# Head 0's gate and value projections interleaved, x staged later: a two-layer retention and latent-attention trunk

## The chip, the cores and the metric

The kernel runs on one core of a Trainium2 chip. The metric is the device time of one execution in microseconds (us), the median of several runs. A separate execution is recorded by the hardware profiler; all views of the profile come from that one. Five engines work side by side, each in its own order: TensorE (PE in the profile, with PEld for its weight loads), VectorE (DVE), ScalarE (ACT), GpSimd (POOL) and SyncE (SP), which issues most of the DMA transfers.

## What is computed

A trunk of two layers over 256 positions with 2048 features, all in float32. Layer one is retention with 8 heads and a squared-ReLU MLP, layer two is multi-head latent attention (MLA) with 16 heads over one shared set of keys and values, and a second MLP. The part that the change touches is the start of the retention and the end of the shared keys:

```python
h = rms_norm(x, norm_mix[layer])
proj = h @ w_in
q, k, v, gate = jnp.split(proj, ...)              # 8 heads: q, k of 256, v, gate of 512
q, k = apply_rope(q, ...), apply_rope(k, ...) * dk ** -0.5
o = ...                                           # decayed causal q k^T v, per head
o = o * lax.rsqrt(jnp.mean(o * o, axis=-1, keepdims=True) + RMS_EPS)
x = x + (jax.nn.silu(gate) * o) @ w_out
...
kv = (c_kv @ w_kv_up).reshape(b, s, MLA_HEADS, MLA_NOPE_DIM + MLA_V_DIM)
k_nope = rms_norm(kv[..., :MLA_NOPE_DIM], k_nope_norm)
```

## The kernel before

**Tiling.** The 256 positions are two row tiles of 128 (`t`), the 2048 features are 16 row blocks of 128 (`k`), paired into 8 chunks (`c`, two blocks `j` each). To keep float32 precision every operand is split into a high and a low part: ScalarE casts the high part (`split`, L191, or with a scale L194) and VectorE subtracts it to get the low one (L192, L195). A product then takes three matmuls: high by high, high by low, low by high (L252 to L254 for plain GEMMs, L376 to L378 for the later ones).

**Weights.** `stream` (L214) loads a 1 MB piece of a weight matrix into a `raw` tile (4 buffers), splits each half of it into `wh` and `wl` (5 buffers each) and hands the half to `use`, which issues the matmuls. `piece` (L241) does that for plain GEMMs, `gemm_t` (L261) for the transposed queries and keys, `gemm_pair` (L351) for the big ones.

**Normalisation.** The row factor of the first norm, `r0`, is applied after the projections, so they can start on the raw, transposed x (`xt`) times the gain. `first_inputs` (L592) loads one chunk of `xt` and splits it; chunks 2, 4, 5 and 7 are loaded again later for sums (`again`, L602). `load_x` (L620) loads x itself in blocks of 512 columns, takes the sum of squares on ScalarE and writes the block to its place in HBM (`x_home`) by a DMA that GpSimd issues.

**The order of head 0.** `gemm(..., "rg0", gated, start)` (L777) makes the gates over all 16 row blocks. It is given `start` (L627): before each half piece of weights one chunk of `xt` is loaded, for the first halves between two parts of the weight load. With half 3 also positions, constants (`cst`, 672 columns) and `gpe` are loaded, with half 5 GpSimd begins the rope tables (`ret_tables`, L570), with half 7 the loads of x and `scale_tables` (L574) are queued. Then `ret_projected` (L728) makes the queries (`rq0`) and the keys (`rk0`), and a second `gemm` makes the values (`rv0`, L779). `gated` copies the gates' sums to SBUF (L767) and applies the Silu 8 steps later; the values are read from PSUM by `ret_valued` (L739).

**What sets the order.** Work that isn't on the matmul path is put in a queue: `later(n, fn)` (L99) runs `fn` when the clock, which `tick` raises by one after each weight piece, has gone on by n. The rotation of queries and keys (`ret_rope`, L640), the scores (`ret_scores`, L660), the outputs (`ret_out`, L681) and the table transposes (`tr_tp`, L585) are timed in this way. Below that, the tile framework orders each engine's instructions by its own plan and puts in the waits: `gqn` (L1037) stands near the end of the code and runs at 4.56 us. Tiles of one tag share their buffers: `acc` has four PSUM banks (one GEMM takes two, L426), `f2k` 14 SBUF buffers.

**The last keys.** `keys(b)` (L1030) makes one eighth of the keys and values of MLA; seven are made before the queries, the eighth after them (L1160), and right behind it comes the output projection `wo` (L1165). `keyed` (L1000) empties the two accumulators with four ScalarE instructions (L1010, L1011), 128x256 each, scaled by `rc`.

Of the kernel before, what the change touches and what calls it, by code (L numbers as in the profile page):

```python
# [21 lines left out]
NT = 2  # L22
# [46 lines left out]
def yoco(ctx: ExitStack, tc: tile.TileContext, a):  # L69
# [144 lines left out]
    def stream(w, chunk, cols, name, use, done=None, before=None):  # L214

        raw = pool.tile([P, 2048], F32, tag="raw", bufs=4, name=f"{name}_raw")
        if before is None:
            nc.sync.dma_start(raw[:, :cols], w[chunk])
        n = cols // 2
        for half in range(2):  # L220
            wh = pool.tile([P, 1024], F32R, tag="wh", bufs=5, name=f"{name}_wh{half}")
            wl = pool.tile([P, 1024], F32R, tag="wl", bufs=5, name=f"{name}_wl{half}")
            cuts = 1
            if before is not None:
                cuts = 1 if half else 2
                m = n // cuts
                for i in range(cuts):
                    lo = half * n + i * m
                    nc.sync.dma_start(raw[:, lo : lo + m], w[chunk][:, lo : lo + m])
                    if i == 0:  # L230
                        before(half)
# [9 lines left out]
    def piece(w, chunk, acc, act, g, nk, nb, name, before=None, done=None):  # L241

        if before is None:
            need(act, 2 * g + 2)

        def use(half, wh, wl):
            for j in range(2):
                k = g * 4 + half * 2 + j
                rh, rl = (v[:, j * nb : (j + 1) * nb] for v in (wh, wl))
                for t in range(NT):  # L250
                    ah, al = (act[k // 2][:, j, i, t * P : (t + 1) * P] for i in range(2))
                    nc.tensor.matmul(acc[t], ah, rh, start=k == 0, stop=False)  # L252
                    nc.tensor.matmul(acc[t], ah, rl, start=False, stop=False)
                    nc.tensor.matmul(acc[t], al, rh, start=False, stop=k == nk - 1)  # L254

        stream(
            w, chunk, 4 * nb, f"{name}{g}", use, done and (lambda: done(acc)),
            before and (lambda half: before(2 * g + half)),
        )
# [169 lines left out]
    def gemm(w, chunk0, act, nk, nb, name, done, before=None):  # L429
# [3 lines left out]
        for g in range(n - 1):  # L433
            piece(w, chunk0 + g, acc, act, g, nk, nb, name, before)
        last_piece(w, chunk0, acc, act, nk, nb, name, done, before)

    def last_piece(w, chunk0, acc, act, nk, nb, name, done, before=None):
        g = nk // 4 - 1
        piece(w, chunk0 + g, acc, act, g, nk, nb, name, before, done)
# [64 lines left out]
    def sincos(inv, w, name, pos_f=pos_f):  # L504
# [37 lines left out]
        def finish(zero):  # L542
            sc = f2k([2, n], f"{name}_sc")
            nc.scalar.activation(sc, r, AF.Sin, bias=zero)
# [25 lines left out]
    def ret_tables():  # L570
        nc.vector.tensor_copy(pos_f, pos_i)
        ret_sc.append(sincos(cst[:, C_INVR : C_INVR + 128], 128, "tr"))

    def scale_tables():  # L574
# [4 lines left out]
        sc = ret_sc[0](zero)  # L579
# [10 lines left out]
    act0, sums0, r0, ret_sc, mla_sc, no_turn = [], [], [], [], [], []  # L590

    def first_inputs(c):  # L592

        t = f2k([2, S], f"x0t_{c}")
        nc.sync.dma_start(t, a["xt"][:, 2 * c : 2 * c + 2, :])
# [4 lines left out]
        if c in HEAD:  # L600
# [12 lines left out]
            later({2: 21, 4: 14, 5: 15, 7: 17}[c], again)  # L613
# [6 lines left out]
    def load_x(b):  # L620
        for t in range(NT):
# [3 lines left out]
            nc.gpsimd.dma_start(x_home[t][b], x0)  # L625

    def start(half):  # L627
        first_inputs(half)
        if half == 3:
# [3 lines left out]
        if half == 5:  # L633
            ret_tables()
        if half == 7:
            for b in range(NB):
                later(2 + b, lambda b=b: load_x(b))
            later(6, scale_tables)

    def ret_rope(acc, out, name, wait):  # L640

        u = f2k([2, S], f"{name}_u")
        for i in range(2):
# [37 lines left out]
    def ret_out(h, s, v, gate, y_act):  # L681
# [17 lines left out]
        if h == 0:  # L699
# [5 lines left out]
            later(25, mla_tables)  # L705
# [22 lines left out]
    def ret_projected(h, qk, gate, v, s):  # L728

        wait = 0 if h else 8  # L730

        def keyed(acc):
            ret_rope(acc, qk, f"rk{h}", max(wait - 4, 0))
            later(max(wait - 4, 0) + (2 if h else 1), ret_scores(h, qk, s))

        gemm_t(a["ret_w_qk"], h * 2, act0, KD, f"rq{h}", lambda acc: ret_rope(acc, qk, f"rq{h}", max(wait - 2, 0)))
        gemm_t(a["ret_w_qk"], (RH + h) * 2, act0, KD, f"rk{h}", keyed)

    def ret_valued(src, h, s, v, gate):  # L739
# [5 lines left out]
        later(1, lambda: ret_out(h, s, v, gate, halves[h // 4]))  # L745
# [14 lines left out]
    for h in range(RH):  # L760
        qk, gate, v, s = [], [], [], []
        if h == 0:

            def gated(acc, gate=gate):
                src = [f2k([512], f"gate_raw{t}") for t in range(NT)]
                for t in range(NT):
                    nc.scalar.copy(src[t], acc[t])  # L767

                def silu():
                    for t in range(NT):  # L770
                        g = f2k([512], f"gate0{t}")
                        nc.scalar.activation(g, src[t], AF.Silu, scale=r0[t])
# [6 lines left out]
            gemm(  # L779
                a["ret_w_gv0"], 4, act0, KD, 512, "rv0",  # L780
                lambda acc, v=v, s=s, gate=gate: ret_valued(acc, 0, s, v, gate),
            )
# [217 lines left out]
    def keyed(acc, b):  # L1000
# [6 lines left out]
        for t in range(NT):  # L1007
            src = acc[t].rearrange("p (h c) -> p h c", h=2)
            k = f2k([2, 2, NOPE], f"kn{b}{t}")
            nc.scalar.activation(k[:, 0], src[:, :, 0:NOPE], AF.Copy, scale=rc[t])  # L1010
# [260 lines left out]
```

## Time and profile before

| | |
|---|---|
| median of 3 runs | 2458.53 us (2458.52 to 2459.41) |
| the profiled execution | 2459.33 us, its span 2457.5 us |
| mean granted TensorE clock | 0.999 |
| busy | TensorE 100%, VectorE 90%, ScalarE 66%, GpSimd 10% |
| DMA | 522.10 MB, 212 GB/s over the span |
| first matmul of head 0's gates | 5.66 us |
| gates, then queries begin, values begin | 31.34, 53.92 us |

The span runs from the first to the last instruction; the time also holds what lies around it. In a timeline row stand the start, the busy time, engine, line, operation, output and inputs by the program's names, the count, and in brackets how long the engine had been idle before it and what released it. A row of the windows view has the stretch and its length, then for PE, PEld, DVE, ACT and POOL the busy time and the number of instructions, then the granted clock, the busy share of the DMA engines and their rate in GB/s; asked for one line of the code, only the engine that runs it is listed. A row of the waits view has the engine and line that waited, what for, the total, the times and the longest. Matmuls are pipelined: their durations overlap, and the distance of their starts is what one costs.

### The profile page before, as it was taken

The page shows a single profiled execution, that of the slowest core. Times are in us where ns is not written, and L with a number is a line of the kernel's source. Part 1 is how long each engine was busy: PE and PEld are TensorE (multiplying, and loading weights), DVE is VectorE, ACT ScalarE, POOL GpSimd, SP SyncE. Part 2 cuts the span into 40 slices and gives each one's busy share as a digit, 9 for nine tenths or more (in the row PEclk, how much of TensorE's full clock was granted, in tenths as well). Part 3 has the DMA queues.
Part 4 walks back from the last instruction along what each step waited for, and adds up shares of the span by engine and source line. Part 5 has one row for each costly group of instructions (what it writes and reads, how often), then busy time and mean ns, then how long its engine had stood idle before and what let it go on. Part 6 is the DMA issues. An engine that isn't in the chain of part 4 may idle for free.

```text
span 2457.5 us, 31830 instructions
## 1 busy us (share of the span) xinstructions
PE 2448.9 (100%) x11620; PEld 2057.4 (84%) x11620; DVE 2220.2 (90%) x2893; ACT 1629.1 (66%) x2300; POOL 250.0 (10%) x311
## 2 busy tenths in 40 slices
PE   9999999999999999999999999999999999999999
PEld 7888888888888888888888888998888888888887
DVE  7799999889899999999999998777999999999998
ACT  6566656566676667667666777676776666676665
POOL 7300011000010010110110001110000101101101
PEclk9999999999999999999999999999999999999999
DMA  9545568555564685674785565445555856857856
GB/s 335 207 174 208 189 208 244 193 183 216 201 237 178 211 261 212 208 257 180 242 271 202 183 223 184 156 150 180 206 189 197 259 212 208 271 197 226 262 188 188
DMA packets 93980, 522.10 MB, mean 212 GB/s; under 512 B 11136, under 2 KB 12288, under 8 KB 40576
## 3 DMA queue, kind: packets, MB, share of 16 engines
q1 hardware_dynamic: 70992, 471.25, 53.2%
q0 software_dynamic: 22400, 48.25, 9.1%
q8 instruction: 91, 1.49, 0.2%
q10 hardware_dynamic: 432, 0.57, 0.1%
q14 instruction: 65, 0.53, 0.1%
HBM read 479.14 MB, written 41.94 MB: 212 GB/s over the span
## 4 chain that ended last, share of the span: by engine, by line
PE 99%; ACT 0%; DVE 0%; DMA 0%; issue 0%; POOL 0%; SPq 0%; ACTq 0%; POOLq 0%
PE u_c L376 7%; PE u_c L378 7%; PE u_c L377 7%; PE d_c L376 7%; PE d_c L378 7%; PE d_c L377 7%; PE rp_c L376 3%; PE rp_c L377 3%; PE rp_c L378 3%; PE rk_acc L280 2%; PE rq_acc L280 2%; PE u_p L376 2%; PE u_p L377 2%; PE u_p L378 2%; PE d_p L376 2%; PE d_p L377 2%
## 5 line engine op out<-in xcount | busy, mean ns | idle before, releaser
L191 ACT CAST u_wh<-u_raw 128x1024 fp32r<-128x1024 f32 x360 | 345.9, 992 | 197.7 <-DVE u_raw L339 95.6
L191 ACT CAST d_wh<-d_raw 128x1024 fp32r<-128x1024 f32 x342 | 327.5, 990 | 185.4 <-DVE d_raw L339 93.9
L192 DVE TENSOR_TENSOR u_wl<-u_raw,u_wh 128x1024 fp32r<-128x1024 f32 x360 | 400.1, 1146 | 36.4 <-ACT u_wh L191 31.3
L192 DVE TENSOR_TENSOR d_wl<-d_raw,d_wh 128x1024 fp32r<-128x1024 f32 x342 | 378.5, 1142 | 30.8 <-ACT d_wh L191 26.2
L376 PE MATMUL u_c<-u_wh,n 128*128 128x512 f32 x712 | 278.8, 392 | 0.0
L377 PE MATMUL u_c<-u_wl,n 128*128 128x512 f32 x712 | 277.8, 390 | 0.0
L378 PE MATMUL u_c<-u_wh,n 128*128 128x512 f32 x712 | 277.4, 390 | 0.0
L376 PE MATMUL d_c<-d_wh,hid 128*128 128x512 f32 x654 | 256.0, 391 | 0.0
L377 PE MATMUL d_c<-d_wl,hid 128*128 128x512 f32 x654 | 255.3, 390 | 0.0
L378 PE MATMUL d_c<-d_wh,hid 128*128 128x512 f32 x654 | 254.8, 390 | 0.0
L191 ACT CAST rp_wh<-rp_raw 128x1024 fp32r<-128x1024 f32 (+1 forms) x166 | 158.8, 981 | 128.1 <-DVE rp_raw L339 65.2
L192 DVE TENSOR_TENSOR rp_wl<-rp_raw,rp_wh 128x1024 fp32r<-128x1024 f32 (+1 forms) x166 | 184.1, 1137 | 18.4 <-ACT rp_wh L191 16.5
L378 PEld LDWEIGHTS u_c<-u_wh,n 128*128 128x128 f32 x712 | 133.7, 188 | 27.7
L376 PEld LDWEIGHTS u_c<-u_wh,n 128*128 128x128 f32 x712 | 133.7, 188 | 27.2
L377 PEld LDWEIGHTS u_c<-u_wl,n 128*128 128x128 f32 x712 | 133.8, 188 | 26.7
L378 PEld LDWEIGHTS d_c<-d_wh,hid 128*128 128x128 f32 x654 | 122.8, 188 | 25.4
L376 PEld LDWEIGHTS d_c<-d_wh,hid 128*128 128x128 f32 x654 | 122.8, 188 | 25.0
L377 PEld LDWEIGHTS d_c<-d_wl,hid 128*128 128x128 f32 x654 | 122.9, 188 | 24.6
L156 POOL DMA_DIRECT2D xh<-d_c x52 | 45.1, 867 | 925.5 <-ACT d_c L396 923.6
L191 ACT CAST ro_wh<-ro_raw 128x1024 fp32r<-128x1024 f32 x88 | 85.6, 996 | 59.4 <-DVE ro_raw L339 25.2
L376 PE MATMUL rp_c<-rp_wh,a 128*128 128x512 f32 x286 | 111.8, 391 | 0.0
L377 PE MATMUL rp_c<-rp_wl,a 128*128 128x512 f32 x286 | 111.3, 389 | 0.0
(584 smaller groups left out, 6177.8 us busy)
## 6 DMA issues: line engine op xcount, KB each, us to landing
u_raw<-in_mlp_w SPq DMA_DIRECT2D x128, 1024.0 KB, 5.3
d_raw<-in_mlp_w SPq DMA_DIRECT2D x120, 1024.0 KB, 4.9
rp_raw<-in_ret_w_gv SPq DMA_DIRECT2D x56, 1024.0 KB, 4.9
ro_raw<-in_ret_w_out SPq DMA_DIRECT2D x32, 1024.0 KB, 4.9
uq_raw<-in_mla_w_uq SPq DMA_DIRECT2D x24, 768.0 KB, 4.1
rq_raw<-in_ret_w_qk SPq DMA_DIRECT2D x16, 1024.0 KB, 4.8
rk_raw<-in_ret_w_qk SPq DMA_DIRECT2D x16, 1024.0 KB, 5.2
wo_raw<-in_mla_w_o SPq DMA_DIRECT2D x16, 1024.0 KB, 4.9
```

The costliest lines, as they stand in the source:

```text
L156: nc.gpsimd.dma_start(x_home[t][2 * p + j], part, accum_op=ALU.add)
L191: nc.scalar.copy(h, src)
L192: nc.vector.tensor_tensor(l, src, h.bitcast(F32), op=ALU.subtract)
L280: nc.tensor.matmul(acc[f], wh[:, cols], a.rearrange("p i s -> p (i s)"), start=k == 0, stop=k == nk - 1)
L376: nc.tensor.matmul(dst, ah, bh, start=n == 0, stop=False)
L377: nc.tensor.matmul(dst, ah, bl, start=False, stop=False)
L378: nc.tensor.matmul(dst, al, bh, start=False, stop=n == total[key] - 1)
```

## The change

Four things are done.

1. Head 0's gates and values are made in one pass over the 8 chunks. Their weights are laid out anew on the host: chunk c holds 256 rows, gates first, then values. `start(c, raw)` now loads both weights and x of a chunk: for chunk 0 x comes in two halves with weight pieces of 512 columns between and behind them, and its splits are cut in two; for the others the order is gate weights, x, value weights. All four accumulator banks are in use; both results are copied to SBUF by ScalarE (`raws`), Silu and values follow 5 and 4 steps later. The queries and keys come after.
2. Positions and the first 160 columns of the constants are loaded after chunk 1, the rest after chunk 3; the rope tables begin with chunk 2, and their first conversion runs on GpSimd. The sine waits for the queries' sums (`first_u`). The loads of x for the squares are queued from chunk 3 on.
3. x isn't written to its place in HBM then; it is loaded once more in head 2 and written from there (`load_home`).
4. In the eighth `keyed` VectorE empties the accumulators.

Some waits of the queue are set anew with it.

```diff
-    def stream(w, chunk, cols, name, use, done=None, before=None):
+    def stream(w, chunk, cols, name, use, done=None, load=None):
         raw = pool.tile([P, 2048], F32, tag="raw", bufs=4, name=f"{name}_raw")
-        if before is None:
+        if load is None:
             nc.sync.dma_start(raw[:, :cols], w[chunk])
+        else:
+            load(raw)
...
+            cuts = 2 if load and chunk == 0 else 1
...
+    def rows_256(acc, v, wh, wl, nb, first, last):
+        for j in range(2):
+            rh, rl = (w[:, j * nb : (j + 1) * nb] for w in (wh, wl))
+            for t in range(NT):
+                ah, al = (v[:, j, i, t * P : (t + 1) * P] for i in range(2))
+                nc.tensor.matmul(acc[t], ah, rh, start=first and j == 0, stop=False)
+                nc.tensor.matmul(acc[t], ah, rl, start=False, stop=False)
+                nc.tensor.matmul(acc[t], al, rh, start=False, stop=last and j == 1)
...
-        def finish(zero):
+        def finish(zero, late=None):
             sc = f2k([2, n], f"{name}_sc")
+            if late is not None:
+                nc.scalar.copy(sc[:, 0, 0:1], late)
...
-        nc.vector.tensor_copy(pos_f, pos_i)
+        nc.gpsimd.tensor_copy(pos_f, pos_i)
...
-        sc = ret_sc[0](zero)
+        sc = ret_sc[0](zero, first_u[0][:, 0, 0:1])
...
-            later({2: 21, 4: 14, 5: 15, 7: 17}[c], again)
+            later({2: 22, 4: 10, 5: 10, 7: 12}[c], again)
...
             square_sum(x0, ss0[t][:, b : b + 1], f"n0_{t}{b}")
-            nc.gpsimd.dma_start(x_home[t][b], x0)
+    def load_home(b):
+        for t in range(NT):
+            x0 = f2k([512], f"xh_{t}{b}")
+            nc.sync.dma_start(x0, x_in(t, b))
+            later(1, lambda t=t, x0=x0: nc.gpsimd.dma_start(x_home[t][b], x0))
+    def start(c, raw):
+        def weights(lo, hi):
+            nc.sync.dma_start(raw[:, lo:hi], a["ret_w_gv0"][c][:, lo:hi])
+        if c == 0:
+            first_inputs(c, weights)
+            weights(1024, 1536)
+            weights(1536, 2048)
+        else:
+            weights(0, 1024)
+            first_inputs(c)
+            weights(1024, 2048)
+        if c == 1:
             nc.sync.dma_start(pos_i, a["pos"])
-            nc.sync.dma_start(cst, a["cst"])
+            nc.sync.dma_start(cst[:, :C_MASK], a["cst"][:, :C_MASK])
+        if c == 2:
+            ret_tables()
+        if c == 3:
+            nc.sync.dma_start(cst[:, C_MASK:], a["cst"][:, C_MASK:])
             nc.sync.dma_start(gpe, a["gpe"])
             for b in range(NB):
-                later(2 + b, lambda b=b: load_x(b))
-            later(6, scale_tables)
+                later(1 + b, lambda b=b: load_x(b))
+                later(23 + 2 * b, lambda b=b: load_home(b))
+            later(7, scale_tables)
...
+            both = [accs(512, name) for name in ("rg0", "rv0")]
+            def raws(v=v, s=s, gate=gate):
+                src = [[f2k([512], f"{name}_raw{t}") for t in range(NT)] for name in ("gate", "v")]
+                for i in range(2):
+                    for t in range(NT):
+                        nc.scalar.copy(src[i][t], both[i][t])
...
-                later(8, silu)
-            gemm(a["ret_w_gv0"], 0, act0, KD, 512, "rg0", gated, start)
+                later(5, silu)
+                later(4, lambda: ret_valued(src[1], 0, s, v, gate, 4))
+            for c in range(KD // 2):
+                def use(half, wh, wl, c=c):
+                    rows_256(both[half], act0[c], wh, wl, 512, c == 0, c == KD // 2 - 1)
+                stream(
+                    a["ret_w_gv0"], c, 2048, f"gv{c}", use, raws if c == KD // 2 - 1 else None,
+                    lambda raw, c=c: start(c, raw),
+                )
             ret_projected(h, qk, gate, v, s)
-            gemm(
-                a["ret_w_gv0"], 4, act0, KD, 512, "rv0",
-                lambda acc, v=v, s=s, gate=gate: ret_valued(acc, 0, s, v, gate),
-            )
...
-            nc.scalar.activation(k[:, 0], src[:, :, 0:NOPE], AF.Copy, scale=rc[t])
-            nc.scalar.activation(vt[:, t], src[:, :, NOPE:], AF.Copy, scale=rc[t])
+            for dst, part in ((k[:, 0], src[:, :, 0:NOPE]), (vt[:, t], src[:, :, NOPE:])):
+                if b < 7:
+                    nc.scalar.activation(dst, part, AF.Copy, scale=rc[t])
+                else:
+                    nc.vector.tensor_scalar(dst, part, rc[t], None, op0=ALU.mult)
```

More of the change, by code (lines that the diff above doesn't have):

```diff
@@ L222, in stream @@
             wl = pool.tile([P, 1024], F32R, tag="wl", bufs=5, name=f"{name}_wl{half}")
[L223 to L231, printed above, removed]
+            cuts = 2 if load and chunk == 0 else 1
             m = n // cuts
@@ L427, in accs, with gemm @@
         return [bank("acc", [nb], f"{name}_acc{t}") for t in range(NT)]
-    def gemm(w, chunk0, act, nk, nb, name, done, before=None):
+    def gemm(w, chunk0, act, nk, nb, name, done):
         acc = accs(nb, name)
@@ L744, in ret_valued @@
             v.append((vh, vl))
-        later(1, lambda: ret_out(h, s, v, gate, halves[h // 4]))
+        later(wait, lambda: ret_out(h, s, v, gate, halves[h // 4]))
     def ret_out_half(i):
```

65 lines of the change are left out of this document (25 added, 40 removed).

## The prediction, made before the result was known

> **What bounds the kernel now.** I read the busy shares and the waits of TensorE over the whole run first, then the timeline and the granted clock of the first 32 us, then the place of the one late wait. Fences hold the rows picked.
>
> ```profile
> span 2457.5 us, 31830 instructions
> PE 2448.9 (100%) x11620; PEld 2057.4 (84%) x11620; DVE 2220.2 (90%) x2893; ACT 1629.1 (66%) x2300; POOL 250.0 (10%) x311
> PE rg_acc L252 <- ACT a L194: 2.1, 2, 1.4
> PE idle L133 <- DVE zeros L130: 1.2, 1, 1.2
> PE wo_c L376 <- ACT v L1011: 1.0, 1, 1.0
> ```
>
> The three wait rows are all that TensorE (PE) waits for: 4.3 us in 2457.5. PE is the bound everywhere, so the change can win only what PE loses in the places it touches: the first matmuls (`rg_acc`) and the first matmuls after the last keys (`wo_c`). It can lose anywhere that it makes a new wait. Now the start, as PE's rows and the granted clock show it:
>
> ```profile
> 5.66 0.50 PE L252 MATMUL rg_acc<-rg_wh,a 128*128 128x512 f32 x1 [0.68 <-ACT a L194]
> 8.37 0.40 PE L254 MATMUL rg_acc<-rg_wh,a 128*128 128x512 f32 x1
> 10.16 0.73 PE L252 MATMUL rg_acc<-rg_wh,a 128*128 128x512 f32 x2 [1.40 <-ACT a L194]
> ...
> 15.00 0.39 PE L252 MATMUL rg_acc<-rg_wh,a 128*128 128x512 f32 x1
> ...
> 31.34 0.61 PE L280 MATMUL rq_acc<-a,rq_wh 128*128 128x512 f32 x2
> 4.59:8.00 3.41, 2.73 (x12) 1.77 (x11) 2.32 (x5) 1.82 (x4) 0.00 (x0) 1.00 0.95 287
> 8.00:11.41 3.41, 1.90 (x8) 0.88 (x7) 1.68 (x3) 2.75 (x6) 0.00 (x0) 1.00 1.04 401
> 11.41:14.83 3.42, 3.42 (x10) 2.74 (x9) 3.42 (x6) 2.79 (x6) 0.00 (x0) 0.51 1.04 382
> ```
>
> Durations overlap, so I go by starts. From 15.00 to 31.34 run 72 matmuls: 16.34/72 = 0.227 us each. All 96 matmuls of the gates would take 21.8 us; they take 31.34 - 5.66 = 25.7. **The start loses 3.9 us.** Part is the hole from 8.6 to 10.16, where a step's 12 matmuls (2.7 us) are done before the next weights and x have landed. Part is the clock (the column behind the engines): 0.51 from 11.41 to 14.83, after a stretch in which PE was busy 1.90 of 3.41 us; after one with 2.73 busy it stayed at 1.00.
>
> **Gates and values in turn.** Removed: the two separate passes. Added: steps with 24 matmuls for each x chunk, 24 x 0.227 = 5.45 us, where there were 12 and 2.7 us. The matmuls are the same 192, so only their waits change. What a step needs from the others stands in these rows, picked from the windows and the engines' timelines:
>
> ```profile
> 10.00:20.00 10.00, 9.72 (x34) 7.60 (x35) 9.25 (x17) 8.31 (x17) 3.85 (x5) 0.83 1.02 351
> 4.56 0.15 DVE L1037 TENSOR_SCALAR gqn<-gains 128x1 f32<-128x1 f32 x1 [3.43 <-DMA gains<-in_gains]
> 5.10 0.91 ACT L194 ACTIVATE a<-x0t,gains 128x256 fp32r<-128x256 f32 x2
> 5.91 0.60 ACT L191 CAST rg_wh<-rg_raw 128x512 fp32r<-128x512 f32 x1
> 8.66 1.04 ACT L191 CAST rg_wh<-rg_raw 128x1024 fp32r<-128x1024 f32 x1 [2.14 <-DMA rg_raw<-in_ret_w_gv]
> 9.73 1.23 DVE L192 TENSOR_TENSOR rg_wl<-rg_raw,rg_wh 128x1024 fp32r<-128x1024 f32 x1 [2.49 <-ACT rg_wh L191]
> 12.62 1.04 ACT L191 CAST rg_wh<-rg_raw 128x1024 fp32r<-128x1024 f32 x1 [0.29 <-DMA rg_raw<-in_ret_w_gv]
> 5.03 0.69 DVE L192 TENSOR_TENSOR rg_wl<-rg_raw,rg_wh 128x512 fp32r<-128x512 f32 x1 [0.32 <-ACT rg_wh L191]
> L195 DVE SCALAR_TENSOR_TENSOR a<-x0t,gains,a x16: 473/480/1512, 5.6 to 26.4; 128x256 fp32r<-128x256 f32 x16
> ```
>
> A step moves 1.25 MB (1.31 million bytes): at 351 GB/s 3.7 us, with 0.5 MB of x beside it 5.2, both under 5.45. Hence DMA binds only the first two steps. The landings there: 1329 KB had been asked for when the row at 8.66 began, 2865 KB at 12.62: 388 KB/us. The new first step asks for the same 1329 KB (49 of gains, 256 of x, 1024 of weights), so it is all there by about 8.66; the next gate weights (1841 KB) by 10.0, their x (2097) by 10.6.
>
> First step: x's first half scaled at 4.56 (gains) to 5.06, the first weight piece cast (0.60) to 5.6, so the first matmul starts at 5.66 as now. ScalarE may do x's second half first; then it starts 0.45 later. VectorE makes x's low part (0.47) and then the weights' low part (0.69), to 6.35; the second matmul, due at 5.89, starts then: **0.45 us lost**. Then 23 x 0.227 run to 11.6, with the later pieces in time. Second step: cast 10.0 to 11.0, x to 11.5, low weights 12.3, low x 12.7; the third matmul, due at 12.0, starts at 12.75: **0.75 lost**. From then on landing gains some 1.7 us a step on PE. Loss 1.2 in place of 3.9: **2.7 us won**, at full clock.
>
> The clock could not stay full. In 4.59 to 8.00 PE would be busy some 2.3 us (3.41 less 0.68 before the first matmul and 0.45 behind it), between the 2.73 that held the clock and the 1.90 that lost it. If it drops, the stretch costs 3.42 x 0.5 = 1.7 and hides the second step's 0.75: 0.9 more in all. The trace leaves this open; 2.3 is as near to the one as to the other, and I take full clock since the weak stretch ends in dense matmuls. The Trainium skill ("TensorE: Matmul & The Clock Gate", Part 1) has a free-running window of 3.413 us that gates the clock after an idle window, and warns of idle gaps over some 3 us. The stretch of 3.42 us agrees; the gap does not, since here 1.4 us was enough. By the page's gap rule there is no drop in the new start and the sum stands; by this trace it may.
>
> **The other engines beside it.** ScalarE has per step two casts (2.1), x (0.9) and for four steps two squares (1.6): 4.6 of 5.45. The raw copies of the values, two of 0.59, are new:
>
> ```profile
> 30.85 1.27 ACT L767 COPY gate_raw<-rg_acc 128x512 f32<-128x512 f32 x2 [4.03 <-PE rg_acc L254]
> 15.91 1.84 POOL L513 TENSOR_SCALAR tr_ang<-cst,pos_f 128x128 f32<-128x128 f32 x2 [15.07 <-DVE pos_f L571]
> 55.77 4.53 POOL L625 DMA_DIRECT2D xh<-x  x8
> 62.95 0.72 ACT L544 ACTIVATE tr_sc<-tr_rr,no_turn 128x512 f32<-128x512 f32 x1 [1.01 <-POOL no_turn L577]
> 33.10:49.40 16.30, 15.69 (x9) 1.00 0.80 276
> 24.93 2.27 DVE L195 SCALAR_TENSOR_TENSOR a<-x0t,gains,a 128x256 fp32r<-128x256 f32 x2
> 38.03 7.51 DVE L192 TENSOR_TENSOR rk_wl<-rk_raw,rk_wh 128x1024 fp32r<-128x1024 f32 x4
> ```
>
> All four accumulator banks are taken. The queries (`rq`) need the gates' two, whose last matmul comes 12 x 0.227 = 2.7 us before the stage ends; the copies take 1.27, so the banks are free 1.4 us ahead. If another cast (1.05) stands before them on ScalarE, still 0.4. Behind the copies on ScalarE stand the queries' next casts, which PE needs through VectorE; a query half lasts 2.8 us on PE, and one or two are cast ahead. Cost nothing; without that cover, up to 1.3.
>
> GpSimd (POOL) works at the tables from 15.91 to 55.77, 39.9 us. In the new order positions and constants come after the second step and POOL begins at about 12.5, ends near 53, and lacks the eight issues (4.53) that move to head 2. The sine now waits for the queries' sums, at about 50.5 + 11.3 + 1 = 63, the transposes stand behind the keys at 73: 7 us of slack or more. Behind the waiting sine on ScalarE stand casts of the keys, which run up to five halves (13 us of PE) ahead. No PE wait. The conversion moved from VectorE to POOL (0.16) counts for nothing in either. The later times of the rotations, scores and outputs are the queue's, with slack of a whole half-head.
>
> VectorE beside a busy POOL is slower: nine low parts in 15.69 us, 1.74 each. A step then takes 2 x 1.74 + 2 x 0.55 = 4.6 of 5.45: kept hidden. Its worst rows are the rival below.
>
> **x in head 2.** The eight loads of 256 KB are made twice (2 MB more), the writes move to head 2. DMA there is half idle, and SP's weight loads behind them are buffered four chunks deep:
>
> ```profile
> 160.00:180.00 20.00, 20.00 (x109) 17.24 (x108) 17.75 (x29) 9.66 (x17) 2.26 (x4) 1.00 0.54 196
> ```
>
> 2.1 million bytes over four steps of about 5 us is 105 GB/s beside 196, under the 351 above. On GpSimd two issues at a time (4.53/8 = 0.57 each) can stand ahead of a head's output factor, 1.1 us late for work that PE takes two weight steps later: nothing.
>
> **The last keys.** The bank that `wo_c` needs is freed by four ScalarE reads that stand behind softmax work:
>
> ```profile
> 1675.57 0.39 PE L378 MATMUL wo_c<-wo_wh,ot 128*128 128x512 f32 x1
> 1676.99 0.50 PE L376 MATMUL wo_c<-wo_wh,ot 128*128 128x512 f32 x1 [1.04 <-ACT v L1011]
> 1674.74 1.48 ACT L1125 ACTIVATE p<-p,inv 128x128 f32<-128x128 f32 x4
> 1676.13 0.45 ACT L1010 ACTIVATE kn<-ku_acc,ck_r 128x256 f32<-128x256 f32 x1
> 1674.05 0.26 DVE L904 TENSOR_TENSOR qu<-qu 128x128 f32<-128x128 f32 x1
> 1674.86 1.23 DVE L192 TENSOR_TENSOR wo_wl<-wo_raw,wo_wh 128x1024 fp32r<-128x1024 f32 x1 [0.56 <-ACT wo_wh L191]
> 1678.53 0.29 DVE L1070 TENSOR_TENSOR qpp<-qu,qpp 128x128 fp32r<-128x128 f32 x1
> 45.47 0.74 DVE L645 TENSOR_TENSOR rq_u<-rq_acc,rq_u 128x256 f32<-128x256 f32 x2
> ```
>
> The hole is 1676.99 - 1675.80 = 1.2 us. VectorE idles at 1674.3; a read of PSUM of this size costs it 0.4 (0.74 for two). From 1674.3 the bank is free at 1675.1; behind the low part at 1674.86, at 1676.9, nothing won. Against it: 1.6 us more of VectorE ahead of `qpp` (done 1678.8 now), whose transposes come due at 1679.0 once the hole is gone; that could give back 0.2 to 1. I take **1.0 won**, between 0 and 1.2, nearer the idle stretch.
>
> **Sum.** 2.7 + 1.0 = 3.7 us. The profiled execution took 2459.33 (its span and 1.8 around it): 2455.6. It lies 0.8 above the median of the three runs (2458.53); if those 0.8 are of the run and not of the start, the median falls to 2454.8. I keep 2455.6 and leave 0.8 to the range. Against the median that is -0.12%. A measurement of this kernel tells about 0.2% (4.9 us) from no change.
>
> **Rivals.** (1) *The clock drops in the new start too*: +0.9, 2456.5. For: 2.3 busy is under 2.73; against: over 1.90. (2) *The change doesn't shorten the start*: the bytes of the first two steps land as slowly as between 5.9 and 8.66 throughout, and the old 3.9 come back: 2458.3. Against: 388 KB/us from 8.66 on. (3) *VectorE becomes the bound beside POOL, and the kernel is slower*: at the worst rows a step costs it 2 x 1.88 (7.51/4) + 2 x 1.13 (2.27/2) = 6.0 us. It decides from 5.45 on; over seven steps (6.0 - 5.45) x 7 = 4.0: 2459.6, above the median before. For: POOL is busy through the whole stage; against: the mean rows give 4.6. The Trainium skill ("SBUF — State Buffer", Who interferes with whom) says that a VectorE instruction with two SBUF inputs and a GpSimd one that reads SBUF share one read port, and that the later one blocks fully; the low parts have two such inputs, and the 1.74 beside 1.23 agrees. (4) *Late tables or scores*: a PE wait behind the keys for the table transposes. It needs the 40 us of POOL to become 57, or tiles to run out where gates, values and x reloads are held together; each us costs one, 2461 and up. (5) *A gain of 4.9 or more*: all losses gone, and the 0.8 too: 2453.5.
>
> **How the numbers follow.** Forecast (2454.6 to 2456.2) 0.45; clock 0.22; start not shorter 0.10; VectorE 0.10; late tables 0.07, nearly all of it beyond 0.2%; larger gain 0.06. The range reaches from 2454.0 to 2459.7: it leaves out the larger gain, the late tables and a part of the VectorE case. Faster by over 0.2% 0.06, slower 0.06, within 0.88.
>
> **What would show it.** Right: no hole near 9 us; short PE waits after the first matmul and near 12 us; the gates and values done 45 us after the first matmul; no wait at `wo_c`; the rest as before. Wrong: a granted clock near 0.5 behind 8.0 (rival 1); PE waits for `a` or the weights after 15 us, named VectorE (3) or DMA (2); a wait at `tr_tp`, `sc` or `o` between 60 and 100 us (4); a wait before `qptp` near 1678.

## The result and the profile after

The changed kernel takes 2464.05 us (median; 2462.09 to 2465.51), the kernel before, run beside it, 2459.24 (2458.25 to 2460.73). The ratio is 1.0018, with a 95% interval of 1.0012 to 1.0024: slower by 4.8 us. Foretold was 2455.6, faster by too little to be told, with a range up to 2459.7.

The profiled execution of the changed kernel has a span of 2461.7 us, 4.2 more than before. First the page's head and TensorE's waits (engine, line and tile that waited, who released it, total, times, longest):

```profile
span 2461.7 us, 31850 instructions
PE 2450.0 (100%) x11620; PEld 2057.1 (84%) x11620; DVE 2222.3 (90%) x2894; ACT 1629.4 (66%) x2297; POOL 255.8 (10%) x312
PE qptp L211 <- DVE qpp L1103: 2.4, 1, 2.4
PE ytp L211 <- DVE st L695: 1.6, 1, 1.6
PE idle L133 <- DVE zeros L130: 1.2, 1, 1.2
PE wo_c L370 <- DVE v L1044: 1.1, 1, 1.1
PE rv_acc L241 <- ACT gv_wh L191: 0.6, 1, 0.6
PE rv_acc L242 <- DVE gv_wl L192: 0.2, 1, 0.2
```

The waits of the start have shrunk from 2.1 us to 0.8, as hoped. But `wo_c` waits as long as before, now for VectorE, and two waits are new: `ytp`, the transposes of head 0's outputs, and `qptp`, the transposes of the eighth query. Both are released by VectorE.

Where the time went shows in the starts of TensorE's first matmuls of each stage. The kernel before, then after:

```profile
76.21 0.39 PE L280 MATMUL rq_acc<-a,rq_wh 128*128 128x512 f32 x1
145.93 0.39 PE L280 MATMUL rq_acc<-a,rq_wh 128*128 128x512 f32 x1
1774.79 0.39 PE L376 MATMUL u_c<-u_wh,n 128*128 128x512 f32 x1
```

```profile
4.93 0.51 PE L241 MATMUL rg_acc<-gv_wh,a 128*128 128x512 f32 x1
8.85 0.50 PE L241 MATMUL rv_acc<-gv_wh,a 128*128 128x512 f32 x1 [0.60 <-ACT gv_wh L191]
73.47 0.48 PE L274 MATMUL rq_acc<-a,rq_wh 128*128 128x512 f32 x1
111.75 0.60 PE L211 MATMUL ytp<-cst,y 128*128 128x128 f32 x4
115.34 0.66 PE L211 MATMUL ytp<-cst,y 128*128 128x128 f32 x4 [1.60 <-DVE st L695]
145.17 0.39 PE L274 MATMUL rq_acc<-a,rq_wh 128*128 128x512 f32 x1
1676.46 0.47 PE L370 MATMUL wo_c<-wo_wh,ot 128*128 128x512 f32 x1 [1.07 <-DVE v L1044]
1679.80 0.27 PE L211 MATMUL qptp<-cst,qpp 128*128 128x128 f32 x1
1683.15 0.55 PE L211 MATMUL qptp<-cst,qpp 128*128 128x128 f32 x3 [2.39 <-DVE qpp L1103]
1778.54 0.39 PE L370 MATMUL u_c<-u_wh,n 128*128 128x512 f32 x1
```

Head 1 begins 2.74 us sooner (76.21 to 73.47). Head 2 begins only 0.76 sooner: 2.0 us are lost in head 1, where `ytp` waits. The second layer's MLP (`u_c`) begins 3.75 us later: nearly all of the rest, 4.3 us, is lost between the last keys and there, where `qptp` waits. In this execution a stretch at half clock followed that wait (windows of the changed kernel: stretch, length, then PE, PEld, DVE, ACT and POOL busy, granted clock, DMA share, GB/s):

```profile
1680.46:1683.87 3.41, 1.02 (x6) 0.66 (x5) 3.00 (x6) 1.49 (x4) 3.41 (x7) 0.96 0.51 155
1683.87:1687.28 3.41, 3.41 (x10) 2.69 (x9) 0.97 (x2) 0.45 (x1) 0.18 (x1) 0.54 0.90 306
```

Why `qpp` is late stands in VectorE's timeline of the changed kernel:

```profile
1674.30 1.23 DVE L192 TENSOR_TENSOR wo_wl<-wo_raw,wo_wh 128x1024 fp32r<-128x1024 f32 x1 [0.55 <-ACT wo_wh L191]
1675.45 0.48 DVE L1044 TENSOR_SCALAR kn<-ku_acc,ck_r 128x256 f32<-128x256 f32 x1
1675.84 0.48 DVE L1044 TENSOR_SCALAR v<-ku_acc,ck_r 128x256 f32<-128x256 f32 x1
...
1680.87 0.76 DVE L1051 TENSOR_TENSOR kn<-kn,kn_r 128x256 f32<-128x256 f32 x2 [0.91 <-POOL kn_r L181]
1681.55 0.22 DVE L1102 CAST qpp<-qu 128x128 fp32r<-128x128 f32 x1
1681.68 1.22 DVE L192 TENSOR_TENSOR wo_wl<-wo_raw,wo_wh 128x1024 fp32r<-128x1024 f32 x1
1682.82 0.28 DVE L1103 TENSOR_TENSOR qpp<-qu,qpp 128x128 fp32r<-128x128 f32 x1
```

The plan puts the low part of a weight piece (1674.30) ahead of the emptying, so the bank is free no sooner than ScalarE freed it. And the second row tile's `qpp`, done at 1678.8 before, now stands behind instructions that wait for GpSimd's `kn_r` and behind two more low parts (at 1678.75, among the rows left out, and at 1681.68): it is done at 1683.1.

The other place, head 1, in VectorE's timeline of the changed kernel:

```profile
111.44 1.21 DVE L192 TENSOR_TENSOR rp_wl<-rp_raw,rp_wh 128x1024 fp32r<-128x1024 f32 x1
112.58 0.95 DVE L192 TENSOR_TENSOR a0s_more<-a0s_sum,a0s_more 128x512 fp32r<-128x512 f32 x1
113.45 1.30 DVE L192 TENSOR_TENSOR rp_wl<-rp_raw,rp_wh 128x1024 fp32r<-128x1024 f32 x1
114.68 0.41 DVE L694 TENSOR_TENSOR st<-sc,dec 128x256 f32<-128x256 f32 x1
115.01 0.28 DVE L695 TENSOR_TENSOR st<-sc,dec 128x128 f32<-128x128 f32 x1
```

Head 1's scores (`sc`, 110.44 to 111.9) and head 0's two transposes now stand on the same step of the queue. The three tiles share the two PSUM banks of the tag `tp`; the second `ytp` waits until VectorE has read the scores, 2.8 us after they were done, behind low parts and sums.

### The profile page after: what moved, and what is told of

Its sections match the earlier page's. It is cut to its first block, busy times and chain, and to the rows that moved or that the text cites. A ratio compares the mean times of both kernels' runs of the same rounds, so it can differ in the third digit from the quotient of the medians.

```text
span 2461.7 us, 31850 instructions
## 1 busy us (share of the span) xinstructions
PE 2450.0 (100%) x11620; PEld 2057.1 (84%) x11620; DVE 2222.3 (90%) x2894; ACT 1629.4 (66%) x2297; POOL 255.8 (10%) x312
## 4 chain that ended last, share of the span: by engine, by line
PE 98%; DVE 1%; ACT 0%; DMA 0%; issue 0%; POOL 0%; SPq 0%; POOLq 0%; ACTq 0%
PE u_c L372 7%; PE u_c L370 7%; PE u_c L371 7%; PE d_c L372 7%; PE d_c L370 7%; PE d_c L371 7%; PE rp_c L370 3%; PE rp_c L372 3%; PE rp_c L371 3%; PE rq_acc L274 2%; PE rk_acc L274 2%; PE u_p L372 2%; PE u_p L370 2%; PE u_p L371 2%; PE d_p L370 2%; PE d_p L371 2%
## 5 line engine op out<-in xcount | busy, mean ns | idle before, releaser
L370 PE MATMUL rp_c<-rp_wh,a 128*128 128x512 f32 x286 | 111.9, 391 | 0.0
L372 PE MATMUL rp_c<-rp_wh,a 128*128 128x512 f32 x286 | 111.3, 389 | 0.0
```

What stands on the lines that cost most here:

```text
L370: nc.tensor.matmul(dst, ah, bh, start=n == 0, stop=False)
L372: nc.tensor.matmul(dst, al, bh, start=False, stop=n == total[key] - 1)
```

## The experiments

The theory at the outset: the start won what was foretold; the loss is two separate things, VectorE's new order at the last keys, and the collision of `ytp` with `sc`. The rivals: the plan shifted as a whole; VectorE has too much work in these places, whatever the order; the sums over x that were moved forward, or GpSimd's table chain, make it late.

All medians, with the difference to the kernel before that ran beside each, and two lengths from the profiles: head 1 (its first `rq_acc` to that of head 2) and from the first `wo_c` to the first `u_c` of layer two, both by TensorE's starts. An interval of these ratios reaches about 0.09%, 2.2 us, to each side, so a size of 1 us is read from the profiles, not from the medians. The two lengths repeat: in the five profiles in which head 1 is as in the changed kernel it takes 71.67 to 71.74 us, and with ScalarE emptying the last keys the other takes 101.69 to 101.74.

| kernel | median, us | to before, us | ratio (95%) | head 1, us | `wo_c` to `u_c`, us |
|---|---|---|---|---|---|
| before | 2459.24 | | | 69.72 | 101.72 |
| after | 2464.05 | +4.81 | 1.0018 (1.0012 to 1.0024) | 71.70 | 106.03 |
| e1 | 2460.67 | +1.66 | 1.0008 (0.9999 to 1.0017) | 71.74 | 101.70 |
| e2 | 2462.37 | +3.36 | 1.0013 (1.0004 to 1.0022) | 69.71 | 104.39 |
| e3 | 2462.39 | +3.38 | 1.0015 (1.0006 to 1.0023) | 70.70 | 104.41 |
| e5 | 2465.30 | +6.29 | 1.0026 (1.0015 to 1.0037) | 71.67 | 107.05 |
| e4 | 2458.74 | 0.00 | 0.9999 (0.9990 to 1.0008) | 70.49 | 101.74 |
| e10 | 2459.98 | +1.24 | 1.0006 (0.9997 to 1.0014) | 71.68 | 101.87 |
| e6 | 2460.01 | +1.27 | 1.0003 (0.9995 to 1.0012) | 71.68 | 101.70 |
| e11 | 2458.70 | -0.04 | 0.9998 (0.9989 to 1.0007) | 70.44 | 101.69 |
| e7 | 2459.38 | +0.08 | 1.0000 (0.9991 to 1.0009) | 70.45 | 101.73 |
| e8 | 2460.63 | +1.33 | 1.0004 (0.9995 to 1.0013) | 71.50 | 101.72 |
| e13 | 2458.36 | -0.94 | 0.9994 (0.9985 to 1.0003) | 70.46 | 101.74 |
| e14 | 2458.24 | -0.33 | 0.9998 (0.9989 to 1.0007) | 70.47 | 101.69 |

**e1: the last keys on ScalarE again**

```diff
-                if b < 7:
+                if b < 8:
```

> The changed kernel with the fourth part undone: ScalarE empties the eighth keys' accumulators again. Theory (the last keys' work on VectorE pushes the second qpp back, and TensorE waits 2.4 us at qptp and then runs a stretch at half clock): both losses go, the hole at wo_c is again about 1.2 us, and the time falls by the 4.3 us that TensorE lost there, 2464.05 to about 2459.8. Rival (the loss there comes from the other parts, by a plan that shifted as a whole): qptp still waits 2 us or more and the time stays at about 2464.

It came to 2460.67. `qptp` doesn't wait, `wo_c` waits 1.0 us, and the stretch from `wo_c` to `u_c` is again as long as before (101.70 and 101.72). The theory holds. That 3.4 us came back and not 4.3 is within what the medians can't tell apart; e2 shows what the 4.3 is made of.

**e2: the kernel before with the fourth part alone**

```diff
-            nc.scalar.activation(k[:, 0], src[:, :, 0:NOPE], AF.Copy, scale=rc[t])
-            nc.scalar.activation(vt[:, t], src[:, :, NOPE:], AF.Copy, scale=rc[t])
+            for dst, part in ((k[:, 0], src[:, :, 0:NOPE]), (vt[:, t], src[:, :, NOPE:])):
+                if b < 7:
+                    nc.scalar.activation(dst, part, AF.Copy, scale=rc[t])
+                else:
+                    nc.vector.tensor_scalar(dst, part, rc[t], None, op0=ALU.mult)
```

> The kernel before with the fourth part alone: VectorE empties the eighth keys' accumulators. Theory: the same wait at qptp and the same stretch at half clock appear without any of the other parts, so the time rises by about 4.3 us, 2459.2 to 2463.5. Rival (the part does harm only in the plan of the whole change): between 1 us faster and no change, 2458.2 to 2459.2, with no wait at qptp.

It is 3.36 us slower than the kernel before, so the part does its harm alone. The same wait stands in its timeline, but no half clock behind it in its windows:

```profile
1683.62 0.55 PE L211 MATMUL qptp<-cst,qpp 128*128 128x128 f32 x3 [2.37 <-DVE qpp L1073]
```

```profile
1680.46:1683.87 3.41, 1.04 (x6) 0.56 (x6) 2.53 (x6) 1.83 (x3) 3.41 (x6) 1.00 0.38 109
1683.87:1687.28 3.41, 3.41 (x18) 2.85 (x17) 1.44 (x2) 1.60 (x2) 0.64 (x2) 1.00 0.94 323
```

The same hole cost 2.7 us of TensorE here and in e3 (104.39 and 104.41 less 101.72), and 4.3 in the profile of the changed kernel (106.03). The 1.6 us between them are the clock, which drops after the hole in some executions and not in others. The medians lie between (3.4 here; from +4.8 to +1.7, so 3.1, between the changed kernel and e1).

**e3: head 0's transposes one step later**

```diff
-        later(2, turn)
+        later(2 if h else 3, turn)
```

> The changed kernel with head 0's output transposes (ytp) one queue step later, so that they no longer stand on the same step as head 1's scores. Theory (three transpose tiles at one step for two banks): the wait of 1.6 us before ytp goes, and 2.0 us come back, 2464.05 to about 2462. Rival (VectorE is late there because of the sums over x that were moved forward, whatever the step): the wait stays or turns up at the next use of such a bank, and the time stays at about 2464.

2462.39, and the wait at `ytp` is gone. But head 1 is only 1.0 us shorter (70.70), not 2.0: a new row stands in TensorE's waits,

```profile
PE rp_p L371 <- DVE rp_wl L192: 0.6, 1, 0.6
```

So the collision is a cause, and behind it VectorE is late for the next thing: theory and rival each hold for a part.

**e5: the eighth query's transposes one step later**

```diff
-    waits = [(3, 3, 3, 2)] * 4 + [(3, 3, 3, 3), (3, 3, 3, 2)] + [(3, 3, 2, 2), (2, 2, 2, 1)]
+    waits = [(3, 3, 3, 2)] * 4 + [(3, 3, 3, 3), (3, 3, 3, 2)] + [(3, 3, 2, 2), (3, 2, 2, 1)]
```

> The changed kernel with the eighth query's transposes (qptp) one queue step later, VectorE still emptying the last keys' accumulators. Theory (what costs is only that the second qpp comes 3 to 4 us late on VectorE): TensorE has other matmuls in the meantime, the wait of 2.4 us at qptp and the 1.6 us of lower clock go, and about 4 us come back, 2464.05 to about 2460. Rival (VectorE is the late one for everything behind the last keys): the wait moves to the scores of that query or its outputs, and less than 1.5 us come back, 2462.5 or more.

2465.30: slower still, so the theory's number fell. `qptp` no longer waits, but the query's later work does, as the rival had it, though for ScalarE:

```profile
PE wo_p L370 <- ACT ot L191: 2.1, 1, 2.1
...
PE ao L1177 <- ACT pt L1167: 0.9, 1, 0.9
```

Each step of a query is timed from the one before it, so the edit moves the scores, softmax and outputs by a step too. The eighth query is the last, and `wo` needs its outputs: one step later it is too late for them. A late `qpp` can't be hidden in this way; whether the transposes alone could come later wasn't tried.

**e10: the eighth query's `qpp` on GpSimd, the last keys still on VectorE**

```diff
-                nc.vector.tensor_copy(parts[:, :, 0], pe)
-                nc.vector.tensor_tensor(parts[:, :, 1], pe, parts[:, :, 0].bitcast(F32), op=ALU.subtract)
+                split_pe = nc.gpsimd if b == 7 else nc.vector
+                split_pe.tensor_copy(parts[:, :, 0], pe)
+                split_pe.tensor_tensor(parts[:, :, 1], pe, parts[:, :, 0].bitcast(F32), op=ALU.subtract)
```

> The changed kernel, with VectorE still emptying the eighth keys' accumulators, but with the four small instructions that make qpp for the eighth query on GpSimd instead of VectorE. Theory (only qpp's place in VectorE's order costs): the wait of 2.4 us at qptp goes and about 3.4 us come back, 2464.05 to about 2460.6; the hole at wo_c stays at about 1.1 us. Rival (VectorE has too much work there, whatever its order): a wait of 1.5 us or more turns up at qptp or behind it, and the time stays above 2462.5.

2459.98, and all of the loss is back (101.87 against 101.72), though VectorE still empties the accumulators. GpSimd's timeline, and TensorE's:

```profile
1676.04 0.29 POOL L1103 CAST qpp<-qu 128x128 fp32r<-128x128 f32 x1
1676.41 1.31 POOL L1104 TENSOR_TENSOR qpp<-qu,qpp 128x128 fp32r<-128x128 f32 x1
```

```profile
1681.68 0.60 PE L211 MATMUL qptp<-cst,qpp 128*128 128x128 f32 x4
```

`qpp` is done at 1677.7, four microseconds ahead of its transposes, which go through in one piece. So the cause is `qpp`'s place in VectorE's order, not the amount of work there. The edit also takes some 1.0 us of work off VectorE, but its other work doesn't come sooner for it: the first `kn` behind GpSimd's `kn_r` starts 9.5 us after the first `wo_c` (1683.77 less 1674.30), 8.4 in the changed kernel (1680.87 less 1672.51), and nothing waits for it. `wo_c` still waits 1.2 us: with the low part ahead of it, VectorE frees the bank no sooner than ScalarE.

**e4: e1 and e3 together**

> The changed kernel with both repairs together: ScalarE empties the eighth keys' accumulators, and head 0's output transposes come one queue step later. Theory (two separate losses that add up): 2464.05 less 3.4 and 1.7, the two gains measured one by one, 2459.0, level with the kernel before. If the start kept all of the 2.7 us that the profiles show until head 1, it would be 2457. Rival (a third loss of the same origin is still in it): 2460.5 or more.

2458.74, level with the kernel before (0.9999): the two gains add up, and nothing of the start's 2.7 us is seen in the median. The profiles say where it went: the new start wins 1.4 us on average (below), head 1 still takes 0.8 longer than before, and 0.4 to 0.5 are added at the end of the span.

**e6: e1 with GpSimd's second table chain six steps later**

```diff
-            mla_sc.append(sincos(cst[:, C_INVM : C_INVM + 32], 32, "tm", pos))
+            later(6, lambda: mla_sc.append(sincos(cst[:, C_INVM : C_INVM + 32], 32, "tm", pos)))
```

> The changed kernel with ScalarE emptying the eighth keys' accumulators (2460.67) and with GpSimd's second table chain six queue steps later, so that it no longer runs beside head 1's sums on VectorE; the transposes ytp stay where the change put them. Theory (three transpose tiles at one step for two banks, freed by VectorE in its order): the wait before ytp stays at 1 us or more and the time at about 2460.5. Rival (VectorE is late because GpSimd slows it there): the wait shrinks under 0.5 us and the time falls to about 2459.

The wait at `ytp` is 1.6 us as in e1, head 1 as long (71.68). But the edit didn't do what it was meant to do: the plan left the chain where it was. Its first instruction, in GpSimd's timeline of e1 and then of e6:

```profile
105.18 1.81 POOL L507 TENSOR_SCALAR tm_ang<-cst,pos_m 128x32 f32<-128x32 f32 x2
105.42 1.82 POOL L507 TENSOR_SCALAR tm_ang<-cst,pos_m 128x32 f32<-128x32 f32 x2
```

Both stand 31.1 us after head 1 begins. So e6 is e1 once more and leaves the rival untested. What the other traces show: in the kernel before, the same chain runs beside head 1 as well (GpSimd is busy 9.0 of the 10 us from 95 to 105 and 9.1 of the next 10), and no wait comes of it. In the changed kernel, between 107 and 115 us, VectorE's low parts of 128x1024 take 1.21 to 1.30 us; in the kernel before, behind 124 us with GpSimd idle, 1.23. Some shorter instructions do take longer there (the split of a sum, `a0s_more`, up to 0.95 against 0.69; an addition of 128x128, L414, 0.55 against 0.29), by some 0.8 us in all. GpSimd may thus have a share in the 1.6 us; it isn't shown to be the cause, nor ruled out.

**e8: e1 with the sums over x at their old steps**

```diff
-            later({2: 22, 4: 10, 5: 10, 7: 12}[c], again)
+            later({2: 20, 4: 12, 5: 12, 7: 13}[c], again)
```

> The changed kernel with ScalarE emptying the eighth keys' accumulators (2460.67), and with the second loading of the transposed x and its sums at the queue steps that they had before; ytp stays where the change put it. Theory (the collision with head 1's scores is what costs at ytp): the wait before ytp stays over 1 us, 2460.3 or more. Rival (the sums moved forward keep VectorE late): the wait goes, and the time falls by 1.5 us or more, to 2459.2 or less.

Neither was right. The wait at `ytp` goes, so the sums stood in its way; but the time stays, since VectorE is then late for the weights of the output projection:

```profile
PE rp_p L371 <- DVE rp_wl L192: 0.9, 1, 0.9
```

Head 1 lasts 71.50 us, 0.2 less than in e1. So no single piece of VectorE's work is what costs. The change also put head 0's outputs later in head 1: the first `ytp` comes 38.3 us after head 1 begins (111.75 less 73.47), before the change 20.3 (96.52 less 76.21). VectorE's work is bunched there, as the windows of the kernel before and then of the changed kernel show:

```profile
95.00:105.00 10.00, 10.00 (x59) 8.65 (x58) 9.17 (x16) 4.75 (x7) 9.02 (x14) 1.00 0.39 125
105.00:115.00 10.00, 10.00 (x47) 8.34 (x46) 7.12 (x9) 5.63 (x8) 9.07 (x12) 1.00 0.77 271
```

```profile
95.00:105.00 10.00, 10.00 (x49) 8.33 (x47) 5.19 (x8) 4.91 (x9) 2.47 (x7) 1.00 0.44 152
105.00:115.00 10.00, 8.74 (x43) 7.09 (x41) 10.00 (x17) 4.69 (x6) 9.28 (x11) 1.00 0.43 134
```

VectorE is now busy 5.2 of the first 10 us and all of the next 10, before 9.2 and 7.1. In the full stretch the order only chooses who waits.

**e11: e1 with head 0's outputs one step sooner**

```diff
-                later(4, lambda: ret_valued(src[1], 0, s, v, gate, 4))
+                later(4, lambda: ret_valued(src[1], 0, s, v, gate, 3))
```

> The changed kernel with ScalarE emptying the eighth keys' accumulators (2460.67) and with head 0's outputs one queue step sooner, so that their transposes stand one step ahead of head 1's scores instead of on their step. Theory (the collision is what costs): the wait before ytp goes and all of its 2.0 us come back, 2458.7, better than moving it one step later, since VectorE's dense stretch lies behind. Rival (head 0's outputs then wait for the values' split or for their gate): a new wait of 1 us or more at o or ytp, 2460 or more.

2458.70, the number that was expected, but in part by luck: the wait at `ytp` goes, yet only 1.3 of the 2.0 us are back in head 1 (70.44), and 0.4 remain as a wait of `sc` for `y`. In its profile the start went badly, the reason for the next readings: windows first, then the row in TensorE's timeline.

```profile
8.00:11.41 3.41, 1.65 (x6) 0.86 (x5) 1.38 (x2) 1.24 (x2) 0.00 (x0) 1.00 0.99 325
11.41:14.83 3.42, 3.42 (x10) 2.70 (x9) 1.91 (x3) 2.90 (x4) 0.75 (x2) 0.54 1.04 386
```

```profile
9.89 0.50 PE L241 MATMUL rv_acc<-gv_wh,a 128*128 128x512 f32 x1 [1.54 <-ACT gv_wh L191]
```

The value weights began to be cast at 9.22 us, 1.0 later than in the profile of the changed kernel (8.18), TensorE waited 1.54 us, the clock fell to 0.54, and head 1 began at 76.44, later than before the change.

**e7: e11 with x written to its place at once**

```diff
+            nc.gpsimd.dma_start(x_home[t][b], x0)
...
-                later(23 + 2 * b, lambda b=b: load_home(b))
```

> The changed kernel with ScalarE emptying the eighth keys' accumulators, head 0's outputs one queue step sooner (2458.70 with these two), and x written to its place at once as before, not in head 2. What is left of the change is in the main the start. Theory (x in head 2 costs nothing, and the start wins between 0 and 2.7 us, by the execution): no change, 2458.7 within 0.6. Rival (the second loading of x costs what the start wins): 1 us or more faster, 2457.7 or less.

2459.38, 0.08 above the kernel before it, as e11 was 0.04 below: writing x in head 2 neither costs nor wins anything that can be measured (from head 2 to the first `wo_c` 1527.55 us here, 1527.41 in e11).

**e13: e11 with the first chunk's x and value weights in one piece each**

```diff
-            for j in range(2):
-                nc.sync.dma_start(t[:, j], a["xt"][:, j, :])
-                weights(512 * j, 512 * (j + 1))
+            nc.sync.dma_start(t, a["xt"][:, 0:2, :])
+            weights(0, 512)
+            weights(512, 1024)
...
-            weights(1024, 1536)
-            weights(1536, 2048)
+            weights(1024, 2048)
```

> The changed kernel with ScalarE emptying the eighth keys' accumulators and head 0's outputs one queue step sooner (2458.70 with these two), and with the first chunk's x and value weights loaded in one piece each, not two. Theory (the start of the changed kernel waits near 9 us for the third weight piece, since the small pieces move at 224 GB/s): the value weights land by 8.2 us, the waits near 9 us fall under 0.5 us in all, and the time to about 2458. Rival (what the larger piece wins in rate it loses because all of it must have landed): the first matmul of the values waits 1 us or more, no change or slower, 2458.7 or more.

2458.36, 0.94 under the kernel before it; the ratio, 0.9994, can't be told from 1. The waits of its start, from the waits of TensorE:

```profile
PE rg_acc L242 <- DVE gv_wl L192: 0.2, 1, 0.2
PE rg_acc L241 <- ACT a L194: 0.2, 1, 0.2
PE rv_acc L241 <- ACT gv_wh L191: 0.2, 1, 0.2
```

In 4.59 to 8.00 us DMA moved 273 GB/s, against 224 in the changed kernel. The weights began to be cast at 8.54, not by 8.2, and yet the waits are 0.6 us in all, a little over the 0.5 expected. Head 1 begins at 73.36. Its eleven times span 1.1 us (2458.10 to 2459.16), those of e11 3.2.

**e14: e13 with the sums over x at their old steps**

```diff
-            later({2: 22, 4: 10, 5: 10, 7: 12}[c], again)
+            later({2: 20, 4: 12, 5: 12, 7: 13}[c], again)
```

> The kernel of the larger first pieces (2458.36) with the second loading of the transposed x and its sums at the queue steps that they had before. Theory (with the transposes ahead of the scores, what is left in head 1 is the wait of 0.42 us of sc for VectorE's low parts of y, which stand behind those sums): the wait goes, head 1 lasts 0.7 us less, and the time falls to about 2457.7. Rival (VectorE is full through all of head 1's first half, so the work that is moved only makes the next thing late): a wait of 0.4 us or more turns up at rp_c, rp_p or sc, and the time stays at 2458.3 or more.

2458.24, head 1 70.47: the wait of `sc` goes and 0.5 us at `rp_p` comes in its place, so the rival's mechanism was right, though the time is just under its 2458.3. It has the lowest median of all, 0.33 under the kernel before beside it (0.9998; 0.9989 to 1.0007): no version could be told from the kernel before as faster.

## Why the prediction was wrong, step by step

- **What bounds the kernel**: right. TensorE is the bound, and the changes are waits of TensorE or its clock, but for 0.4 to 0.5 us at the very end (see the sum).
- **Gates and values in turn, 2.7 won**: the mechanism is right, the term was mis-sized, and that the one profile of the changed kernel gives 2.74 (76.21 to 73.47) is luck. From the first matmul of the gates to head 1 the kernel before took 70.55 us, and e2, whose start is the old one, 70.56 (5.24 to 75.80): it kept its clock, but TensorE then waited 1.10 us for the queries' low weights. So the old loss was sized about right. The changed kernel took 68.54, which is 2.0 won; the other 0.73 came because its first matmul started at 4.93 us and not "at 5.66 as now".
- **"Loss 1.2 in place of 3.9"**: this is the step of the start that failed, and in it "with the later pieces in time". The gates and values took 45.6 us (4.93 to 50.52), where 192 x 0.227 is 43.6: a loss of 2.0. The cast of the value weights began only at 8.18, and TensorE waited for them near 9 us. In the ten profiles with the new start (the changed kernel, e1 and e3 to e8, e10, e11) that cast began between 7.95 and 9.22, and the way from the first matmul to head 1 took 68.54 to 71.39, 69.65 on average: 0.9 won. Head 1 began between 73.47 and 76.44, 74.6 on average, in the two profiles with the old start at 76.0: 1.4 us won in all, as far as so few tell, not 2.7.
- **The first matmul "at 5.66 as now"**: it came at 4.83 to 5.05 us in these ten. A part of that is the execution: the gains were first used at 4.56 us in the profile before, at 4.10 in e2, at 3.94 to 4.15 in the ten. A part is the halved first piece of x: with x in one piece the first matmul came at 5.24 (e2), 5.15 (e13) and 5.28 (e14), though the gains were as early.
- **The clock in the new start** (rival 1): it holds in nine of the ten profiles with the new start and falls in e11's; with the old start it fell in the profile before and held in e2. So it differs between executions, with either start.
- **Bank release, tables, `tr_tp`**: right. `tr_tp` stands at 73.12 in the changed kernel, without a wait. In six of the ten profiles, though not in the changed kernel's, TensorE waits 0.2 to 0.4 us for the queries' first low weights, where nothing was foretold.
- **"The later times of the rotations, scores and outputs are the queue's, with slack of a whole half-head"**: failed, 2.0 us. What was not looked at is which tiles share the two banks of `tp` at one step, and how full VectorE, which frees them, is in that part of head 1. Three different versions take the wait at `ytp` away (e3, e8, e11), each with a smaller one in its place. GpSimd's share in it stays open (e6). The waiting place was in the list of what would show the prediction wrong only as `sc` or `o`, not as `ytp`.
- **VectorE beside GpSimd**: hidden in the start, as foretold; no wait there after 15 us in the changed kernel names VectorE.
- **x in head 2**: nothing, as foretold (e7 against e11).
- **The last keys, 1.0 won**: this step failed most. Two things in it. The bound "behind the low part ..., nothing won" was the case that came (the low part at 1674.30 goes first, and `wo_c` still waits 1.07). And "1.6 us more of VectorE ahead of `qpp`", priced at 0.2 to 1, was 2.7 us, or 4.3 with the clock: counted were the instructions added ahead of `qpp`, but the plan orders VectorE anew, and `qpp` went behind two low parts and instructions that wait for GpSimd. Its end moved from 1678.8 to 1683.1, by 4.3 us, while the work added is 4 x 0.48 = 1.9 at most. A wait before `qptp` near 1678 stood in the list of signs; it came, at 1680.8 to 1683.2.
- **The sum** for the median: -1.4 (start) + 2.0 (head 1) + 2.7 to 4.3 (last keys) = 3.3 to 4.9. In the profiles another 0.4 to 0.5 us lie behind the last VectorE addition (2453.50 to the end of the span at 2457.5 before, 2457.24 to 2461.7 after); e2 has the old length, e1 and e11 the new. What lengthens it wasn't found. With it the sum is 3.7 to 5.4, against 4.8 measured.

## What to carry to other kernels

When a program orders an engine by a plan, work added to that engine costs its length only if the order stays; look for the instruction with the least slack behind it, and ask what waits it may be put behind, for that is the price and not the added work. When a stage is moved in time, look at the engine that gives back its banks at the new place, not only at the one that uses them. And what the first microseconds of a kernel cost, while the first loads land, needs several executions: the same new start took 68.5 us in one profile and 71.4 in another, a spread as large as the gain that was looked for.

## What the runs showed of the hardware

The clock's answer to a hole depends on the execution. The same wait at `qptp` (2.39 and 2.37 us) dropped the clock to 0.54 for 3.4 us in the changed kernel and left it at 1.00 in e2 and e3. The two starts with 1.65 us of TensorE's work between 8.00 and 11.41 differed as well: e11's fell to 0.54, e2's held:

```profile
8.00:11.41 3.41, 1.65 (x7) 0.74 (x6) 1.49 (x2) 2.57 (x5) 0.00 (x0) 1.00 0.98 346
11.41:14.83 3.42, 3.42 (x16) 2.82 (x16) 3.42 (x7) 2.98 (x6) 0.00 (x0) 1.00 1.07 395
```

So the prediction's measure, busy time in a fixed stretch (2.73 held, 1.90 fell), doesn't decide. The Trainium skill ("TensorE: Matmul & The Clock Gate", Part 1) says that the window is free-running, so that the number of slow matmuls at a kernel's start varies from run to run; different answers to like holes are in keeping with that. Its rule against idle gaps over some 3.4 us is too generous for this case: 1.54 us of wait in e11 was followed by a granted clock of 0.54.

The landing of the same loads moves by more than 1 us between executions: the third weight piece began to be cast at 7.95 us in e5, 8.18 in the changed kernel and 9.22 in e11, all with the same order of loads.
